# A different path for the third of the last four token tiles, and a finer cut of the last one

## The chip, the cores and the metric

The kernel runs on one core of a Trainium2 chip. The metric is the device time of one execution in microseconds. Times "in the span" are counted from the first to the last instruction that the profile holds; the time of an execution is somewhat longer than its span.

## The reference

One encoder layer for 1024 tokens of width 1024, all in 32-bit floats. A projection feeds retention heads and windowed attention heads, their outputs go through `W_out`, and two normalisations close the two halves:

```python
h = _layer_norm(ALPHA * h + mix, ln1_gain[i], ln1_bias[i])
g = jnp.einsum('bsd,df->bsf', h, w_ffn_gate[i].astype(jnp.float32))
up = jnp.einsum('bsd,df->bsf', h, w_ffn_up[i].astype(jnp.float32))
ffn = jnp.einsum('bsf,fd->bsd', jax.nn.silu(g) * up, w_ffn_down[i].astype(jnp.float32))
...
h = _layer_norm(ALPHA * h + ffn + ple_gate * ple, ln2_gain[i], ln2_bias[i])

def _layer_norm(x, gain, bias):
    ...
    return (xf - mu) * lax.rsqrt(var + LN_EPS) * gain.astype(jnp.float32) + bias.astype(jnp.float32)
```

The change concerns only the last line: the second normalisation of some of the tokens, and the stores of its result.

## The kernel before

Tokens lie in eight tiles of 128 (tile t holds one token per partition, 1024 features along it). Each 32-bit matmul is split into three passes (lines 783 to 785). The feed-forward part is computed as a fast matrix product with fewer block products; the last of these products, `(p, s) = (4, 1)`, completes the first halves of tiles 0 to 3. Tiles 4 to 7 are complete earlier, and their normalisation (`ln2_steps`) runs beside the last matmuls.

The order on each engine is the order in which the code is written (a manual schedule for TensorE, VectorE, ScalarE, GpSimd and SyncE). Each engine works off its own queue in that order, and an instruction that waits holds up everything behind it on its engine. Stores are issued by SyncE. Transfers that add to what lies at their destination are issued by GpSimd.

The end of the program is `tail(products)`. For t = 0 to 3 it issues the matmuls of tile t's last half and then works on the normalisation, one stage behind for the tile before. The stages for a tile, with VectorE unless said otherwise:

- `addto` adds the product to the tile's accumulator `accd[t]`; for the last tile (`LAST` = 3) it also takes the half's statistics.
- `var` makes the mean and the variance; for tiles other than the last, ScalarE sums the squares.
- `rstd` adds the epsilon and takes the power -0.5 on GpSimd (line 1632) into column 15 of the tile's small table `stts[t]`.
- `center` subtracts the mean and multiplies by the gain `ln2[0]`, in two halves of 512 columns (line 1637).
- `scale` multiplies by column 15 and adds the bias `ln2[1]`, in two halves (line 1642), with a store behind each (line 1643).

For the last tiles the order is: root of tile 2, sum and statistics of tile 3, root of tile 3, scaling and stores of tile 2, centring of tile 3, scaling and stores of tile 3. `ln2_steps`, for tiles 4 to 7, already knows another way: ScalarE scales the whole tile (line 1654), VectorE multiplies by the gain (line 1657), and a transfer from GpSimd's queue adds the bias (line 1658); one store of the whole tile follows (line 1714).

Of the kernel before, what the change touches and what calls it, by code (L numbers as in the profile page):

```python
# [11 lines left out]
AF = mybir.ActivationFunctionType  # L12
ALU = mybir.AluOpType
# [29 lines left out]
def layer(tc, xT, xn, w_first, w_mt, w_rv, w_out, w_pg, w_pe, pT, w_gu, w_dn,  # L43
          consts, dec_b, dec_c, sink, gng, lnp, out):
    nc = tc.nc
    act, dve, pool, pe, sp = nc.scalar, nc.vector, nc.gpsimd, nc.tensor, nc.sync
# [213 lines left out]
    for h in range(2):  # L260
        sl = slice(h * HF, (h + 1) * HF)
        b = st[1, h]
        for g in range(2):
            a = slice(64 * g, 64 * g + 64)
# [123 lines left out]
    class Retention:  # L388
# [73 lines left out]
        def half(self, hh):  # L462
            return self.y[:, hh * HF:(hh + 1) * HF]
# [206 lines left out]
    def ytile(k):  # L670
        if ys[k] is None:
            ys[k] = a_tile([P, S], "y", "A0" if k < 4 else "A1")
        return ys[k]
# [46 lines left out]
    with tc.manual_schedule(engines={mybir.EngineType.PE}):  # L720
# [7 lines left out]
        a = Attention(0, ytile(1))  # L728
# [16 lines left out]
        for i in range(1, NPAIR):  # L745
# [3 lines left out]
            a = Attention(i, ytile(2 * i + 1))  # L749
# [22 lines left out]
    def ct(shape, tag, bufs=None, dt=F32):  # L772
        return cpool.tile(list(shape), dt, tag=tag, bufs=bufs, name=nm(tag))
# [90 lines left out]
    stts = [ct([P, 16], "stt", 8) for _ in range(NT)]  # L864
# [715 lines left out]
    hs = [slice(h * HF, (h + 1) * HF) for h in range(2)]  # L1580
    accd, R, later = [], [], []
# [24 lines left out]
    LAST = 3  # L1606
# [30 lines left out]
            dve.scalar_tensor_tensor(x, x, stts[t][:, 12:13], ln2[0][:, hs[h]], ALU.add, ALU.mult)  # L1637

    def scale(t):
        for h in range(2):  # L1640
            x = half(t, h)
            dve.scalar_tensor_tensor(x, x, stts[t][:, 15:16], ln2[1][:, hs[h]], ALU.mult, ALU.add)
            sp.dma_start(out[t][:, hs[h]], x)

    def ln2_steps(t):

# [15 lines left out]
    def tail(products):  # L1662

        bs = dbank[len(SEG) - 1, GRP[4]]
        for t in range(4):
            products(t)
            if t:
                rstd(t - 1)
            addto(t, 0, bs[t], done=True)
            var(t)  # L1670
            if t < LAST:
                if t:
                    scale(t - 1)
                center(t)
        rstd(LAST)
        scale(LAST - 1)
        center(LAST)
        scale(LAST)
# [84 lines left out]
    ln2 = []  # L1763
# [191 lines left out]
```

## Time and profile before

| | |
|---|---|
| median of 3 runs | 1173.62 us (1173.25, 1173.62, and one of 4958.54) |
| profiled execution | 1174.31 us |
| its span | 1172.5 us |
| mean granted TensorE clock | 0.998 |
| TensorE busy | 1162.0 us, 99% of the span |
| VectorE busy | 892.2 us, 76% |
| ScalarE busy | 581.0 us, 50% |
| GpSimd busy | 119.5 us, 10% |
| last matmul ends, in the span | 1163.66 us |

In the profile PE is TensorE, DVE VectorE, ACT ScalarE, POOL GpSimd and SP SyncE; "SPq" rows are what SyncE's queue did. A timeline row gives start, duration, engine, line of the kernel, operation, output and inputs, shape and count; in brackets stands the idle time before it and what ended it. Rows of DMA issues end with their median time from issue to landing. The rows that the argument needs stand in the prediction.

### The profile page before, as it was taken

Reading aid. Unit: us, or ns where it says so; the run is one execution under the profiler, and the core shown is the slowest. Engines: PE = TensorE matmul, PEld = TensorE weight load, DVE = VectorE, ACT = ScalarE, POOL = GpSimd, SP = SyncE. Lnnn points to the kernel's source line nnn. Section 1 sums busy time; section 2 is a strip of 40 time slices with the busy share of each in tenths; the row PEclk is TensorE's granted clock in tenths of the full one; section 3 lists DMA queues with packets and bytes.
Section 4 is the critical chain, followed back from the end, with each engine's and each line's share of the span. In section 5 each row is a group of like instructions: output and inputs, shape, how many; then the busy total and the mean of one; then the engine's idle time right before and its main releaser. Section 6 shows DMA issues by size and latency. Waiting matters only on the chain.

```text
span 1172.5 us, 17985 instructions
## 1 busy us (share of the span) xinstructions
PE 1162.0 (99%) x6410; PEld 978.8 (83%) x6410; DVE 892.2 (76%) x1736; ACT 581.0 (50%) x1181; POOL 119.5 (10%) x181
## 2 busy tenths in 40 slices
PE   9999999999999999999999999999999999999996
PEld 7888888888888888888888888888888888888885
DVE  4666678776859788947998988888888976774677
ACT  5566347776756266213444434443344445552463
POOL 2001020202010021000000000000000011134232
PEclk9999999999999999999999999999999999999999
DMA  6345656546346945756323322332223289999977
GB/s 254 95 157 207 243 195 223 207 134 221 110 162 224 385 165 185 279 183 212 117 80 105 123 100 94 112 129 106 100 72 135 85 248 344 348 236 220 259 156 215
DMA packets 80665, 211.76 MB, mean 181 GB/s; under 512 B 9536, under 2 KB 14784, under 8 KB 80576
## 3 DMA queue, kind: packets, MB, share of 16 engines
q1 hardware_dynamic: 71936, 193.84, 47.0%
q0 software_dynamic: 8640, 16.78, 8.3%
q8 instruction: 50, 0.82, 0.3%
q14 instruction: 39, 0.32, 0.1%
HBM read 139.29 MB, written 62.13 MB: 172 GB/s over the span
## 4 chain that ended last, share of the span: by engine, by line
PE 96%; DVE 2%; DMA 1%; issue 1%; ACT 0%; DVEq 0%; POOL 0%; ACTq 0%; POOLq 0%
PE bmm L783 8%; PE bmm L784 8%; PE bmm L785 7%; PE bt L783 6%; PE bt L784 6%; PE bmm L77 6%; PE bt L785 6%; PE bmm L79 6%; PE bmm L78 6%; PE bs L785 4%; PE bs L784 4%; PE bs L783 4%; PE bo L785 3%; PE bo L783 3%; PE bo L784 3%; PE bo L565 2%
## 5 line engine op out<-in xcount | busy, mean ns | idle before, releaser
L77 PE MATMUL bmm<-H,w 128*128 128x512 f32 x240 | 97.5, 406 | 0.0
L79 PE MATMUL bmm<-H,w 128*128 128x512 f32 x240 | 94.1, 392 | 0.0
L78 PE MATMUL bmm<-H,w 128*128 128x512 f32 x240 | 94.0, 392 | 0.0
L1368 ACT ACTIVATE ev<-ev 128x512 f32<-128x512 f32 x42 | 26.4, 630 | 104.3 <-DVE ev L1397 92.8
L1542 POOL DMA_DIRECT2D h0b<-in_w_dn x24 | 21.6, 900 | 539.9 <-PE bt L785 504.6
L77 PEld LDWEIGHTS bmm<-H,w 128*128 128x128 f32 x240 | 45.2, 188 | 10.0 <-ACT H L71 0.8
L79 PEld LDWEIGHTS bmm<-H,w 128*128 128x128 f32 x240 | 45.1, 188 | 10.1
L78 PEld LDWEIGHTS bmm<-H,w 128*128 128x128 f32 x240 | 45.3, 189 | 7.9
L535 ACT ACTIVATE sc<-sc,st 128x385 f32<-128x385 f32 (+1 forms) x64 | 37.1, 584 | 16.6 <-DVE st L533 16.5
L531 DVE CUSTOM_DVE_ANT_0 sc<-cst,bs,skb 128x384 f32<-128x384 f32 (+1 forms) x64 | 34.9, 576 | 8.9 <-PE bs L530 7.7
L1397 DVE TENSOR_TENSOR ev<-ev,bt 128x512 f32<-128x512 f32 x44 | 30.1, 683 | 12.5 <-PE bt L785 12.5
L1348 DVE TENSOR_TENSOR ev<-ev,bs 128x256 f32<-128x256 f32 x63 | 25.6, 418 | 15.5 <-PE bs L785 14.7
L1370 DVE TENSOR_TENSOR ev<-ev 128x512 f32<-128x512 f32 x42 | 29.0, 691 | 10.5 <-ACT ev L1368 9.0
L72 DVE TENSOR_TENSOR w<-raw,w 128x512 fp32r<-128x512 f32 x34 | 23.1, 690 | 17.9 <-ACT w L71 17.7
L783 PE MATMUL bmm<-H,u 128*128 128x512 f32 x92 | 36.2, 393 | 0.2 <-ACT ev L1406 0.2
L784 PE MATMUL bmm<-H,u 128*128 128x512 f32 x92 | 36.1, 392 | 0.0
L785 PE MATMUL bmm<-H,u 128*128 128x512 f32 x92 | 35.8, 389 | 0.0
L541 ACT ACTIVATE sc<-sc,st 128x384 f32<-128x384 f32 (+1 forms) x64 | 34.0, 580 | 0.8 <-DVE st L539 0.8
L526 POOL COPY sc<-skb 128x1 f32<-128x1 f32 x64 | 15.1, 244 | 179.8 <-PE bt L553 159.6
L783 PE MATMUL bmm<-H,w 128*128 128x512 f32 x84 | 32.9, 392 | 0.0
L784 PE MATMUL bmm<-H,w 128*128 128x512 f32 x84 | 32.9, 392 | 0.0
L785 PE MATMUL bmm<-H,w 128*128 128x512 f32 x84 | 32.7, 389 | 0.0
(791 smaller groups left out, 3893.8 us busy)
## 6 DMA issues: line engine op xcount, KB each, us to landing
ad<-ev SPq DMA_DIRECT2D x33, 512.0 KB, 2.7
pgd<-pro SPq DMA_DIRECT2D x28, 512.0 KB, 3.0
raw<-in_w_gu SPq DMA_DIRECT2D x22, 512.0 KB, 3.6
ln<-in_w_gu SPq DMA_DIRECT2D x22, 512.0 KB, 3.9
raw<-ad SPq DMA_DIRECT2D x40, 256.0 KB, 5.9
ln<-ad SPq DMA_DIRECT2D x37, 256.0 KB, 6.3
H<-in_w_dn SPq DMA_DIRECT2D x33, 256.0 KB, 7.8
wod<-aq SPq DMA_DIRECT2D x15, 512.0 KB, 2.7
```

Source lines behind the costliest of these rows:

```text
L77: pe.matmul(o, lh, rh, start=start, stop=False)
L78: pe.matmul(o, lh, rl, start=False, stop=False)
L79: recent[0] = pe.matmul(o, ll, rh, start=False, stop=stop).ins.name
L531: dve.tensor_tensor_reduce(sc[g][:, :nk], cst[:, tc0:tc0 + nk], b[:, :nk], slope(i, g), skb[:, 2 * i + g:2 * i + g + 1], ALU.add, ALU.max, ...
L535: act.activation(sc[g][:, :nk + 1], sc[g][:, :nk + 1], AF.Exp, bias=st_[:, 1, j, g:g + 1], accum_out=st_[:, 2, j, g:g + 1])
L541: behind(act.activation(sc[g][:, :nk], sc[g][:, :nk], AF.Copy, scale=st_[:, 3, j, g:g + 1]))
L783: pe.matmul(o, lh, rh, start=start, stop=False, skip_group_check=True)
L784: pe.matmul(o, lh, rl, start=False, stop=False, skip_group_check=True)
L785: pe.matmul(o, ll, rh, start=False, stop=stop, skip_group_check=True)
L1368: act.activation(c[:, 0, :], c[:, 0, :], AF.Silu)
L1370: dve.tensor_tensor(c[:, 1, :], c[:, 0, :], c[:, 1, :], ALU.mult)
L1397: dve.tensor_tensor(get(name), ev[left][:, m, :], right, ALU.add)
```

## The change

`scale` is rewritten. Tiles 0 and 1 are treated as before. Tile 2 (`t == LAST - 1`) is multiplied by column 15 on ScalarE, whole; a transfer from GpSimd's queue adds the bias; one store of the whole tile follows. Tile 3 is scaled and stored in three pieces of 512, 256 and 256 columns. `tail`, which calls it, is unchanged.

```diff
     def scale(t):
-        for h in range(2):
-            x = half(t, h)
-            dve.scalar_tensor_tensor(x, x, stts[t][:, 15:16], ln2[1][:, hs[h]], ALU.mult, ALU.add)
-            sp.dma_start(out[t][:, hs[h]], x)
+        x = accd[t]
+        if t == LAST - 1:
+            act.activation(x, x, AF.Copy, scale=stts[t][:, 15:16])
+            pool.dma_start(x, ln2[1], accum_op=ALU.add)
+            sp.dma_start(out[t], x)
+            return
+        for a, b in ((0, 512), (512, 1024)) if t < LAST else ((0, 512), (512, 768), (768, 1024)):
+            dve.scalar_tensor_tensor(x[:, a:b], x[:, a:b], stts[t][:, 15:16], ln2[1][:, a:b], ALU.mult, ALU.add)
+            sp.dma_start(out[t][:, a:b], x[:, a:b])
```

Five lines more stand ahead of what follows, so line 1643 is 1648 in the changed kernel and line 1714 is 1719; 1642 to 1644 are the new operation, transfer and store of tile 2.

VectorE at the end of the program (`acc_8954` is tile 2, `acc_8978` tile 3, `u_9952` the gain, `u_9954` the bias):

```order
 L1622 TENSOR_SCALAR stt_3912<-stt_3912 128x1
 L1631 TENSOR_SCALAR stt_3912<-stt_3912 128x1
-L1642 SCALAR_TENSOR_TENSOR acc_8954<-acc_8954,stt_3911,u_9954 128x512 x2
 L1637 SCALAR_TENSOR_TENSOR acc_8978<-acc_8978,stt_3912,u_9952 128x512 x2
-L1642 SCALAR_TENSOR_TENSOR acc_8978<-acc_8978,stt_3912,u_9954 128x512 x2
-L1951 UNCONDITIONAL_BRANCH
+L1647 SCALAR_TENSOR_TENSOR acc_8978<-acc_8978,stt_3912,u_9954 128x512
+L1647 SCALAR_TENSOR_TENSOR acc_8978<-acc_8978,stt_3912,u_9954 128x256 x2
+L1956 UNCONDITIONAL_BRANCH
```

The pair for tile 2 is gone, and the last pair is cut in three.

GpSimd at the end of the program (the four rows at the top are the roots of tiles 0 to 3):

```order
 L1632 TENSOR_TENSOR stt_3909<-stt_3909,cst 128x1
 L1632 TENSOR_TENSOR stt_3910<-stt_3910,cst 128x1
 L1632 TENSOR_TENSOR stt_3911<-stt_3911,cst 128x1
 L1632 TENSOR_TENSOR stt_3912<-stt_3912,cst 128x1
-L1951 UNCONDITIONAL_BRANCH
-L1951 ISA
+L1643 DMA acc_8954<-u_9954 128x1024
+L1956 UNCONDITIONAL_BRANCH
+L1956 ISA
```

The adding transfer for tile 2 stands behind the root of tile 3.

SyncE at the end of the program, before (stores of tile 7 and then of tiles 0 to 3, two halves each):

```order
L1714 DMA out_y<-acc_9110 128x1024
L1643 DMA out_y<-acc_8899 128x512 x2
L1643 DMA out_y<-acc_8926 128x512 x2
L1643 DMA out_y<-acc_8954 128x512 x2
L1643 DMA out_y<-acc_8978 128x512 x2
L1951 UNCONDITIONAL_BRANCH
```

and with the change:

```order
L1719 DMA out_y<-acc_9110 128x1024
L1648 DMA out_y<-acc_8899 128x512 x2
L1648 DMA out_y<-acc_8926 128x512 x2
L1644 DMA out_y<-acc_8954 128x1024
L1648 DMA out_y<-acc_8978 128x512
L1648 DMA out_y<-acc_8978 128x256 x2
L1956 UNCONDITIONAL_BRANCH
```

The store of tile 2 is one, and it stands ahead of the three of tile 3. ScalarE gets the scaling of tile 2 as its last instruction.

## The prediction

> **What bounds the kernel now.** I read the page first, then the end of the timeline engine by engine, then the DMA views of the same stretch, since the change touches only the last steps of the program.
>
> ```profile
> span 1172.5 us, 17985 instructions
> PE 1162.0 (99%) x6410; PEld 978.8 (83%) x6410; DVE 892.2 (76%) x1736; ACT 581.0 (50%) x1181; POOL 119.5 (10%) x181
> PE 96%; DVE 2%; DMA 1%; issue 1%; ACT 0%; DVEq 0%; POOL 0%; ACTq 0%; POOLq 0%
> ```
>
> TensorE is busy for 99% of the span and carries 96% of the chain that ended last. The diff has no matmul in it and nothing that a matmul waits for, so that part keeps its length. What can move is what comes after the last matmul.
>
> ```profile
> 1163.27 0.39 PE L785 MATMUL bs<-u,u 128*128 128x512 f32 x1
> ```
> ```profile
> 1163.69 0.69 DVE L1600 TENSOR_TENSOR acc<-acc,bs 128x512 f32<-128x512 f32 x1 [0.17 <-PE bs L785]
> 1164.41 0.69 DVE L1602 BATCH_NORM_STATS2 stt<-acc 128x6 f32<-128x512 f32 x1
> ...
> 1165.46 0.14 DVE L1631 TENSOR_SCALAR stt<-stt 128x1 f32<-128x1 f32 x1
> 1165.52 1.40 DVE L1642 SCALAR_TENSOR_TENSOR acc<-acc,stt,u 128x512 f32<-128x512 f32 x2
> 1166.84 1.41 DVE L1637 SCALAR_TENSOR_TENSOR acc<-acc,stt,u 128x512 f32<-128x512 f32 x2
> 1168.16 1.41 DVE L1642 SCALAR_TENSOR_TENSOR acc<-acc,stt,u 128x512 f32<-128x512 f32 x2
> ```
>
> The last product ends at 1163.66. From there the end is a chain on VectorE without a gap: the last tile's sum and statistics, then three pairs of half-tile operations: scaling of tile 2 (L1642), centring of tile 3 (L1637), scaling of tile 3 (L1642 again), ending at 1169.57. Behind it stands one store:
>
> ```profile
> 1169.60 0.33 SPq L1643 DMA_DIRECT2D out_y<-acc  x1
> ```
> ```profile
> out_y<-acc SPq DMA_DIRECT2D x2, 256.0 KB, 2.0
> ```
>
> The last half-tile store is issued at 1169.60 and lands 2.0 us later, at 1171.6; the span ends at 1172.5, so 0.9 us lie between the last landing and the end. About 8.8 us of the span follow the last matmul, and this is all that the change can act on. The time of this profiled execution is 1174.31, 1.81 above its span; the median of the runs is 1173.62, 1.12 above the span. I make the sum in the span and add 1.12.
>
> **The change, part by part.** First, what goes. The pair at 1165.52 leaves VectorE. Centring of tile 3 starts where it stood, so all that VectorE does behind it comes 1.32 us earlier (1166.84 less 1165.52). The reciprocal root of tile 3 on GpSimd, which its scaling needs, keeps its place:
>
> ```profile
> 1142.14 0.91 POOL L1658 DMA_DIRECT2D acc<-u  x1 [0.36 <-DVE stt L1630]
> 1142.79 1.92 POOL L1632 TENSOR_TENSOR stt<-stt,cst 128x1 f32<-128x1 f32 x1
> ...
> 1150.32 0.89 POOL L1658 DMA_DIRECT2D acc<-u  x1 [3.17 <-DVE acc L1657]
> 1151.46 0.86 POOL L1658 DMA_DIRECT2D acc<-u  x1 [0.25 <-issue]
> 1163.60 0.54 POOL L1632 TENSOR_TENSOR stt<-stt,cst 128x1 f32<-128x1 f32 x1 [3.53 <-DVE stt L1631]
> 1165.68 0.98 POOL L1632 TENSOR_TENSOR stt<-stt,cst 128x1 f32<-128x1 f32 x1 [1.55 <-DVE stt L1631]
> ```
>
> It ends at 1166.66, and the earlier centring would end at about 1166.9, so it is in time, by 0.2 us. Its 0.98 beside VectorE's pair (against 0.54 for the one at 1163.60) I keep, since VectorE runs the same kind of pair beside it; 0.54 and 1.92 are the bounds, -0.4 and +0.9.
>
> The last scaling is cut into 512, 256 and 256 columns. No row shows this operation at 256 columns; the nearest is
>
> ```profile
> L1348 DVE TENSOR_TENSOR ev<-ev,bs 128x256 f32<-128x256 f32 x63 | 25.6, 418 | 15.5 <-PE bs L785 14.7
> ```
>
> 0.42 us against 0.74 for a half tile. VectorE would end between 1168.3 and 1169.0; I take 1168.4. If the stores followed at once, this alone would bring the end forward by about 1 us.
>
> Second, what comes in its place, and it is on another path. ScalarE scales all of tile 2 in one operation. Like rows and the end of its work before:
>
> ```profile
> 1147.19 1.24 ACT L1654 ACTIVATE acc<-acc,stt 128x1024 f32<-128x1024 f32 x1 [0.93 <-POOL stt L1651]
> ...
> 1161.99 0.18 ACT L1615 ACTIVATION_READ_ACCUMULATOR sg<-acc,stt 128x1 f32 x1
> ```
>
> ScalarE is idle from 1162.2. The operation needs tile 2 centred (1163.2) and tile 2's root (1163.60 + 0.54 = 1164.14), so it runs from 1164.2 to 1165.4. It costs nothing, because the next step is held until 1167 anyway; without that cover it could be 1.6 us later before it counted.
>
> The next step is the adding transfer of the bias into tile 2, issued by GpSimd. It stands in GpSimd's order behind the root of tile 3, although it needs nothing of it. So it cannot start before 1166.66; the rows above show 0.25 to 0.41 us between an operation and such an issue, and I take 0.4: start at 1167.05. How long it takes until it has landed:
>
> ```profile
> L1658 POOL DMA_DIRECT2D acc<-u x4: 859/894/913, 1142.1 to 1151.5; - x4
> DMA to landing us min/median/max: 4.6/4.9/6.7
> ```
> ```profile
> q0 software_dynamic: 124, 0.51, 66.5%
> ```
> ```profile
> 1146.79 0.34 SPq L1714 DMA_DIRECT2D out_y<-acc  x1
> ```
>
> This is the same transfer (the same bias tile, 512 KB, into a tile of the same size), four times. The first, issued at 1142.14, ran with nothing else in flight (in the DMA view of 1142 to 1146 only the software queue moved data) and took 4.6; its tile's store was issued at 1146.79, 4.65 after the adding transfer's issue. The 6.7 is for the fourth, beside stores and the third. What lies beside the new one:
>
> ```profile
> core 0: us, PE busy (x) PEld busy (x) DVE busy (x) ACT busy (x) POOL busy (x), PEclk, DMA share, GB/s
> 1164.20:1165.50 1.30, 0.00 (x0) 0.00 (x0) 1.20 (x5) 0.00 (x0) 0.00 (x0) 1.00 0.00 0
> 1165.50:1166.90 1.40, 0.00 (x0) 0.00 (x0) 1.40 (x5) 0.00 (x0) 0.98 (x1) 1.00 0.00 0
> ```
>
> The DMA engines are empty, and the two stores that would have filled them next are the ones that the change removes. So I take 4.65, with 6.7 as the upper bound: the store of tile 2 is issued at 1167.05 + 4.65 = 1171.70. That is already 2.1 us after the issue of the last store of the kernel before.
>
> The Trainium skill, "DMA: Bandwidth & Descriptors", section "Anatomy of one DMA — SWDGE (gpsimd) path", gives for a transfer issued by GpSimd 2.0 us plus its bytes at 436 GB/s. By that the landing would be an estimated 3.2 us and the end 1.4 us earlier; the four rows of 4.6 and more decide against it for an adding transfer.
>
> Third, the queue behind it. SyncE issues the stores in written order: all of tile 2 first, then the three pieces of tile 3. So the pieces, whose data is ready at 1168.4, wait behind tile 2's semaphore. That SyncE's queue stands still for such a transfer the profile of before shows already:
>
> ```profile
> SPq L1714 <- DMA acc<-u: 36.7, 4, 26.4
> ```
>
> From 1171.70 there are 1 MB to store in four transfers.
>
> ```profile
> L1714 SPq DMA_DIRECT2D out_y<-acc x4: 332/336/338, 1146.8 to 1158.2; - x4
> DMA to landing us min/median/max: 2.7/3.2/4.5
> ```
> ```profile
> raw<-in_pT SPq DMA_DIRECT2D x8, 128.0 KB, 2.5
> ```
>
> A whole tile lands 2.7 us after its issue where nothing is beside it, a half tile 2.0, so 256 KB more cost 0.7. Issues cost 0.33 each and lie ahead of the data, so the bytes set the end: 2.7 for tile 2, 0.7 for the first piece, and 0.35 for each 128 KB piece if the price goes with bytes, 0.7 if it goes with the number of rows, which is as large as for a half tile. I take 0.35: a whole tile's store and a half tile's have the same 128 rows and yet differ by 0.7, so there the bytes carry the price. The last landing is 1171.70 + 2.7 + 0.7 + 0.7 = 1175.8. Bounds: not before the last issue (1172.7) plus 2.0, which is 1174.7, and not after 1176.5 by this reckoning; the 2.5 of a 128 KB load lies between.
>
> The sum: 1175.8 plus the 0.9 behind the last landing gives a span of 1176.7, that is 4.2 us more than 1172.5. With 1.12 added, the time is **1177.8**.
>
> **The rivals.** (a) *The adding transfer's issue is held up by VectorE.* The root under the long VectorE operation took 1.92 instead of 0.54, so VectorE can hold GpSimd up, and VectorE is busy without a gap until 1168.4. If the issue waited for that, it would start 1.3 us later and everything behind it too: span 1178.0, time 1179.1. Against it speaks this row beside the issue at 1150.32:
>
> ```profile
> 1148.70 2.34 DVE L1657 TENSOR_TENSOR acc<-acc,u 128x1024 f32<-128x1024 f32 x2
> ```
>
> That issue ran inside the second of the two long operations and took 0.89, as the undisturbed ones. I give it 0.12. The Trainium skill, "SBUF — State Buffer", section "SBUF: two separate sides", states a rule for this: VectorE operations in a two-port mode keep GpSimd from writing its descriptors, while those with two SBUF inputs block only GpSimd operations that read SBUF. The 1.92 and the 0.89 agree with the second half of it; no row here shows an issue beside a two-port operation.
>
> (b) *The software queue is slow again,* as for its loads with addition:
>
> ```profile
> DMA to landing us min/median/max: 4.1/6.8/9.7
> ```
>
> These are 256 KB each at line L1542, amid a full DMA. With 9.7 instead of 4.6 the span would be 1181.8 and the time 1182.9. The empty DMA engines speak against it: 0.05.
>
> (c) *Not slower: the adding transfer does not decide.* If tile 2's store were away before the pieces of tile 3 are ready, the end would be VectorE's: the last piece is issued at about 1168.6, lands 2.0 to 2.5 later, and the span is 1171.5 to 1172.0, a time of 1172.6 to 1173.1. It decides as soon as the adding transfer lands before about 1168.3, which is 1.3 us after its issue. The shortest such transfer, of half the bytes, speaks against it:
>
> ```profile
> DMA to landing us min/median/max: 3.4/5.7/9.5
> ```
>
> I give it 0.03. That the change does not do what it says is no case here: both new operations and the new order of stores stand on their queues.
>
> **How the numbers follow.** The forecast has 0.78, (a) 0.12, (b) 0.05, (c) 0.03; 0.02 is left for something not seen here. The likeliest gives 1177.8. The bounds of its terms are -0.4 and +0.9 (the root), +2.1 (a landing of 6.7), -1.1 and +0.7 (the stores), with some 0.4 between the median and other runs. The low end, 1175.8, takes the lower bounds of the root and the stores and that 0.4 together; the high end, 1180.6, takes in (a), or a landing of 6.7 with the dearer small stores. A measurement of this kernel can tell about 2%, 23 us, from no change. For a loss of that size the adding transfer would have to take some 24 us, and no case above comes near; a gain of that size is more than all that follows the last matmul. So within 2% has 0.96, slower by more 0.03, faster by more 0.01.
>
> **What would show it right or wrong.** In the profile of the changed kernel: ScalarE's new operation at about 1164.2 for 1.24 us; VectorE ending near 1168.4; GpSimd's adding issue starting at 1167.0 to 1167.1 and landing 4.6 later; four SyncE issues close together from 1171.7, the pieces of tile 3 more than 3 us after VectorE finished them; the last landing near 1175.8. It is wrong if SyncE issues the pieces before tile 2's store, if the adding transfer lands in under 2 us, or if its issue starts only when VectorE is done. A shift of the last matmul's end from 1163.66 would mean that the change acts elsewhere than I say.

## The result and the profile after

The changed kernel takes 1177.79 us (median of 6 runs, 1176.95 to 1179.0), the kernel before 1173.43 beside it (six runs, one of them of 4958.54 and left out of the ratio). The ratio is 1.0035, with a 95% interval of 1.0025 to 1.0045: slower by about 4.1 us, 2.9 to 5.3, clear of the noise but far within 2%. The profiled execution took 1178.98 us.

Here and below I use the **tail**: the span less the end of the last matmul, with the span as the page gives it, to a tenth, so that a difference of 0.1 between two tails says nothing. Before it was 1172.5 less 1163.66, 8.84 us. The first rows are the span and the last matmul of the changed kernel, from its page and its timeline:

```profile
span 1177.2 us, 17987 instructions
```
```profile
1164.03 0.39 PE L785 MATMUL bs<-u,u 128*128 128x512 f32 x1
```

The last matmul ends at 1164.42, so the tail is 12.78 us, 3.94 more. The other 0.76 us of the longer span lie ahead of the tail, where nothing was changed; more on that behind the experiments. The rows of the tail, engine by engine (VectorE, ScalarE, GpSimd, SyncE), from the timeline:

```profile
1166.34 1.42 DVE L1637 SCALAR_TENSOR_TENSOR acc<-acc,stt,u 128x512 f32<-128x512 f32 x2
1167.67 1.54 DVE L1647 SCALAR_TENSOR_TENSOR acc<-acc,stt,u 128x512 f32<-128x512 f32 x3
```
```profile
1164.93 1.15 ACT L1642 ACTIVATE acc<-acc,stt 128x1024 f32<-128x1024 f32 x1 [1.99 <-POOL stt L1632]
```
```profile
1166.45 1.05 POOL L1632 TENSOR_TENSOR stt<-stt,cst 128x1 f32<-128x1 f32 x1 [1.54 <-DVE stt L1631]
1167.46 0.90 POOL L1643 DMA_DIRECT2D acc<-u  x1
```
```profile
1172.08 0.33 SPq L1644 DMA_DIRECT2D out_y<-acc  x1
1172.50 1.89 SPq L1648 DMA_DIRECT2D out_y<-acc  x3
```

VectorE is done 1169.21, that is 4.79 us into the tail instead of 5.91. But no store of tile 3 leaves then: SyncE's queue stands at tile 2's store until 1172.08, and the three pieces leave behind it. The waits of SyncE's queue name the reason (waited for, total, times, longest), and the DMA view of the tail gives the landings (KB each, median time from issue to landing):

```profile
SPq L1644 <- DMA acc<-u: 9.0, 1, 9.0
```
```profile
acc<-u POOLq DMA_DIRECT2D x1, 512.0 KB, 4.6
out_y<-acc SPq DMA_DIRECT2D x1, 512.0 KB, 2.6
out_y<-acc SPq DMA_DIRECT2D x1, 256.0 KB, 3.0
out_y<-acc SPq DMA_DIRECT2D x2, 128.0 KB, 2.7
```

ScalarE's scaling, which the change added, ended 1.4 us before GpSimd's issue and cost nothing.

### The profile page after: what moved, and what is told of

It is laid out like the page before. It is cut to its first block, busy times and chain, and to the rows that moved or that the text cites. A ratio compares the mean times of both kernels' runs of the same rounds, so it can differ in the third digit from the quotient of the medians.

```text
span 1177.2 us, 17987 instructions
## 1 busy us (share of the span) xinstructions
PE 1162.4 (99%) x6410; PEld 979.2 (83%) x6410; DVE 891.5 (76%) x1735; ACT 582.7 (49%) x1182; POOL 120.3 (10%) x182
## 4 chain that ended last, share of the span: by engine, by line
PE 95%; DVE 2%; DMA 1%; issue 1%; ACT 0%; SPq 0%; POOL 0%; DVEq 0%; ACTq 0%; POOLq 0%
PE bmm L783 8%; PE bmm L784 7%; PE bmm L785 7%; PE bt L783 6%; PE bt L784 6%; PE bt L785 6%; PE bmm L77 6%; PE bmm L79 6%; PE bmm L78 6%; PE bs L785 4%; PE bs L784 4%; PE bs L783 4%; PE bo L785 3%; PE bo L783 3%; PE bo L784 3%; PE bo L565 2%
```

## The experiments

The theories: A, tile 2's adding transfer and the order of SyncE's queue behind it set the end. B, the small stores of the cut are what costs. C, VectorE holds up the adding transfer's issue. D came up on the way and concerns the end of the program. All diffs are against the changed kernel unless said otherwise. The tail and the end of the last matmul are those of one profiled execution each; the time is the median of several. The ratios are to runs of the kernel before beside each (medians 1174.11 to 1174.38), so the times go by the ratios and not by the first row:

| run | last matmul ends | tail, us | time, us | ratio to before, 95% interval |
|---|---|---|---|---|
| before | 1163.66 | 8.84 | 1173.43 | |
| before_again | 1163.62 | 8.88 | 1174.3 | one run |
| the change | 1164.42 | 12.78 | 1177.79 | 1.0035 [1.0025, 1.0045] |
| t3_first | 1163.08 | 11.22 | 1176.12 | 1.0018 [1.0008, 1.0028] |
| add_early | 1162.59 | 11.81 | 1177.14 | 1.0024 [1.0015, 1.0034] |
| both_orders | 1162.98 | 10.22 | 1175.78 | 1.0011 [1.0002, 1.0020] |
| no_bias | 1163.77 | 7.83 | 1173.37 | 0.9993 [0.9983, 1.0002] |
| no_cut | 1164.02 | 12.58 | 1178.38 | 1.0037 [1.0024, 1.0050] |
| cut_alone | 1163.92 | 9.48 | 1174.85 | 1.0005 [0.9996, 1.0014] |
| nine_stores | 1163.75 | 9.35 | 1174.59 | 1.0001 [0.9992, 1.0010] |
| cut_eight | 1163.98 | 9.12 | 1174.36 | 1.0002 [0.9993, 1.0011] |
| add_to_hbm | 1163.62 | 9.68 | 1175.11 | 1.0009 [1.0000, 1.0018] |
| half_moved | 1163.99 | 9.41 | 1174.67 | 1.0003 [0.9994, 1.0012] |
| half_two | 1165.82 | 8.88 | 1174.37 | 1.0001 [0.9992, 1.0010] |

**SyncE's order alone (t3_first).**

```diff
-            sp.dma_start(out[t], x)
             return
...
         center(LAST)
         scale(LAST)
+        sp.dma_start(out[LAST - 1], accd[LAST - 1])
```

> Only the order on SyncE's queue is changed against the change: tile 3's three stores are issued ahead of tile 2's. The measure is the tail, from the end of the last matmul to the end of the span: 8.84 us before, 12.78 with the change. Theory A (tile 2's adding transfer and, behind it, SyncE's queue set the end): the three stores leave near 4.9 us into the tail, tile 2's store still waits until about 7.7, lands 2.6 later, and the tail is 11.2, time about 1.6 us below the change. Theory B (the three small stores themselves are what costs): the small stores still cost their time but early, so the same 11.2; it parts from A only in the run without the cut. Theory C (the adding transfer is late because VectorE holds up its issue): no change of the issue, tail as in A.

The tail is 11.22, as expected. The order of the queue was worth 1.56 of the 3.94 us. Tile 2's store is now the last: it leaves 7.63 into the tail, and its 2.7 us and the 0.9 behind it make the rest:

```profile
1170.71 0.33 SPq L1683 DMA_DIRECT2D out_y<-acc  x1
out_y<-acc SPq DMA_DIRECT2D x1, 512.0 KB, 2.7
```

**GpSimd's order alone (add_early).**

```diff
-        rstd(LAST)
         scale(LAST - 1)
+        rstd(LAST)
         center(LAST)
         scale(LAST)
```

> Only GpSimd's order is changed against the change: tile 2's adding transfer is issued ahead of tile 3's root instead of behind it. Theory A: the issue moves from 3.04 us into the tail to about 1.7 (ScalarE's end), everything behind it by as much, tail 11.4 against 12.78; tile 3's root comes some tenths later and is still in time or costs VectorE less than 0.5, which does not show at the end. Theory C (VectorE holds up the issue): the issue of 0.9 us becomes longer or the landing grows beyond 4.6, since VectorE is in its pair for tile 3 then too, and the tail stays above 12.

The tail is 11.81, not 11.4; the gain is 0.97 instead of 1.4. The issue came 0.4 us after ScalarE's end, for which I had allowed nothing, and tile 3's root behind it kept VectorE waiting for 0.46, which does not show at the end:

```profile
1164.66 0.90 POOL L1643 DMA_DIRECT2D acc<-u  x1 [1.59 <-ACT acc L1642]
1165.27 1.08 POOL L1632 TENSOR_TENSOR stt<-stt,cst 128x1 f32<-128x1 f32 x1
```
```profile
1166.39 1.54 DVE L1647 SCALAR_TENSOR_TENSOR acc<-acc,stt,u 128x512 f32<-128x512 f32 x3 [0.46 <-POOL stt L1632]
```

Theory C falls: the issue, here wholly inside VectorE's centring of tile 3, takes 0.90 and the landing 4.6, as in the changed kernel, where VectorE goes from that pair to the scaling.

**Without the adding transfer (no_bias).**

```diff
             act.activation(x, x, AF.Copy, scale=stts[t][:, 15:16])
-            pool.dma_start(x, ln2[1], accum_op=ALU.add)
             sp.dma_start(out[t], x)
```

> Tile 2 gets no bias here: the adding transfer is left out, ScalarE's scaling and the one store stay. Theory A: without the adding transfer VectorE sets the end, 1.3 us earlier than before; the last small store leaves 4.9 us into the tail and lands 2.0 to 2.5 later, tail 7.8 to 8.3 against 8.84 before, time 0.5 to 1 us below the kernel before. Theory B (the small stores cost what VectorE gains): tail 8.8 or more.

The tail is 7.83, 1.0 us below before. So the earlier VectorE does bring the end forward, if nothing stands in SyncE's way; the last small store left 0.14 us after VectorE's end and landed as fast as a half tile's did before:

```profile
1168.69 0.40 SPq L1647 DMA_DIRECT2D out_y<-acc  x1
out_y<-acc SPq DMA_DIRECT2D x1, 128.0 KB, 2.0
```

This kernel leaves out tile 2's bias, so it is no version to use; the whole gain of the change, had the bias been free, is this 1.0 us. In time the ratio 0.9993 fits it but does not tell it from nothing.

**The move alone (no_cut) and the cut alone (cut_alone).** no_cut keeps the move and stores tile 3 in halves; cut_alone keeps the cut and lets VectorE scale tile 2 as before.

```diff
-        for a, b in ((0, 512), (512, 1024)) if t < LAST else ((0, 512), (512, 768), (768, 1024)):
+        for a, b in ((0, 512), (512, 1024)):
```

> Only the move of tile 2 is kept; tile 3 is scaled and stored in two halves as before. Theory A: the move carries the whole loss, tail 12.4 to 12.8 against 12.78 with the change and 8.84 before. Theory B (the cut carries a good part of the loss): tail under 12, 11 if it carries half.

```diff
-        if t == LAST - 1:
+        if t == -1:
             act.activation(x, x, AF.Copy, scale=stts[t][:, 15:16])
```

> Only the cut of tile 3 into three pieces is made; tile 2 is scaled by VectorE and stored in halves as before. Theory A: VectorE takes 0.13 us more for three pieces than for two, the last store has half the bytes (0.35 less) but lands up to 0.5 later than its bytes say: tail 8.5 to 9.2 against 8.84 before, no difference in time. Theory B (the cut costs): tail 9.5 or more.

The move alone has a tail of 12.58, so it carries 3.74 of the 3.94; B falls as the cause of the loss. Its last store, the second half of tile 3:

```profile
1172.57 0.74 SPq L1648 DMA_DIRECT2D out_y<-acc  x1
out_y<-acc SPq DMA_DIRECT2D x1, 256.0 KB, 3.1
```

But the cut alone was not free: 9.48, outside A's 8.5 to 9.2 and at B's bound of 9.5. VectorE ended 0.13 later and SyncE's third issue came behind the second, so the last landing is 0.2 us later; the rest, 0.4, lies behind it. The last store:

```profile
1170.10 0.40 SPq L1648 DMA_DIRECT2D out_y<-acc  x1
out_y<-acc SPq DMA_DIRECT2D x1, 128.0 KB, 2.0
```

That store landed at 1172.1, yet the span ends at 1173.4, 1.3 later and not 0.9. The instructions of the program's end (line 1956, in the kernel before 1951) on SyncE's queue from the last landing on show why (count, ns each, first and last start); first the cut alone, then the kernel before:

```profile
L1956 SPq EVENT_SEMAPHORE  x8: 27/28/28, 1172.1 to 1172.6; - x8
```
```profile
L1951 SPq EVENT_SEMAPHORE  x1: 28/28/28, 1171.6 to 1171.6; - x1
```

SyncE waits for its eight transfer semaphores one after the other, about 0.06 us each. Before, the last store's semaphore was the last in that order and one wait was left when it landed; with one store more the last store seems to come back to the first, and all eight waits follow its landing. That is theory D, and two runs test it.

**The number of stores (nine_stores, cut_eight).** nine_stores is the kernel before with tile 0's first store in two pieces (its diff is against the kernel before); cut_eight is cut_alone, with its line, and tile 0 stored whole (only what it has beyond cut_alone is shown).

```diff
             x = half(t, h)
             dve.scalar_tensor_tensor(x, x, stts[t][:, 15:16], ln2[1][:, hs[h]], ALU.mult, ALU.add)
-            sp.dma_start(out[t][:, hs[h]], x)
+            if t == 0 and h == 0:
+                for q in (slice(0, 256), slice(256, 512)):
+                    sp.dma_start(out[t][:, q], accd[t][:, q])
+            else:
+                sp.dma_start(out[t][:, hs[h]], x)
```

> The kernel before with one edit far from the end: the first half of tile 0 is stored in two pieces, so that the last eight stores become nine. Theory D (the end of the program waits for SyncE's eight transfer semaphores one after the other, 0.06 us each, in a fixed order, and a ninth store comes back to the first of them): the last landing stays near 7.97 us into the tail, and what follows it grows from 0.91 to about 1.33, tail 9.3 against 8.88. Rival (the longer end of the cut runs came from the small last stores): tail 8.9.

```diff
-            sp.dma_start(out[t][:, a:b], x[:, a:b])
+            if t:
+                sp.dma_start(out[t][:, a:b], x[:, a:b])
+        if t == 0:
+            sp.dma_start(out[t], x)
```

> The cut of tile 3 alone, as in the run of that edit, but tile 0 stored whole, so that there are eight stores again. Theory D: what follows the last landing is 0.91 again instead of 1.34, last landing 8.2, tail 9.1 against 9.53. Rival (small last stores): tail 9.5.

Tails of 9.35 and 9.12, and the waits behind the last landing are eight and one:

```profile
L1955 SPq EVENT_SEMAPHORE  x8: 27/28/28, 1171.8 to 1172.2; - x8
```
```profile
L1959 SPq EVENT_SEMAPHORE  x1: 28/28/28, 1172.2 to 1172.2; - x1
```

D holds in both directions: with the ninth store at tile 0, more than 10 us ahead of the end, the tail is 0.5 us longer than before, and without it the cut alone loses 0.36 and costs 0.28. The changed kernel has eight stores for tiles 0 to 3 (two, two, one and three), so it does not pay this. The times show neither difference.

**The kernel before again (before_again).**

> The kernel before once more, for the scatter of its parts: the tail should be 8.84 within 0.1 us, while the end of the last matmul (1163.66 in the first profile, 1164.42 with the change) may move by a microsecond from run to run. If it comes back at 1163.7, the 0.76 us that the changed kernel was later there belongs to the change or to its profiled execution; if it lies between or beyond, it is scatter.

It came back at 1163.62 with a tail of 8.88. In the six profiles without the new GpSimd transfer the last matmul ends between 1163.62 and 1163.98; in the eight with it, between 1162.59 and 1165.82, to both sides of the kernel before. The executions that were not profiled say what the 0.76 is. Those of the changed kernel have spans of 1175.2 to 1177.2, median 1176.0, and the profiled one is among the two longest; half_two's, with 1165.82, was the slowest of its 11 too, 2.15 above its median. If the tail is the same in all of them, as 8.84 and 8.88 suggest for the kernel before, 1163.2 of the changed kernel's median span lie ahead of it, no more than before. So the 0.76 is most likely scatter between executions; why one execution takes longer than another ahead of the tail stays open.

**Versions that might beat both (add_to_hbm, half_moved, half_two, both_orders).** add_to_hbm stores the bias to tile 2's place in the output early and adds the scaled tile onto it:

```diff
             act.activation(x, x, AF.Copy, scale=stts[t][:, 15:16])
-            pool.dma_start(x, ln2[1], accum_op=ALU.add)
-            sp.dma_start(out[t], x)
+            pool.dma_start(out[t], x, accum_op=ALU.add)
             return
...
+                sp.dma_start(out[LAST - 1], ln2[1])
                 while later:
                     pop()
```

and has GpSimd's order of add_early.

> A version that may beat both: the bias is stored into tile 2's place in the output early, and GpSimd's adding transfer puts the scaled tile straight onto it, ahead of tile 3's root; tile 2 needs no store of SyncE's at the end. Theory A: the adding transfer is issued near 1.8 us into the tail and lands 4.6 to 5.5 later, before the last small store of tile 3, which leaves near 5.2; tail 7.8 to 8.5, time 0.3 to 1 us below the kernel before. If adding into memory off the core takes over 6 us, the tail is 8.8 or more and nothing is won.

The tail is 9.68, a miss. The adding transfer took 5.4, as allowed for, and had landed in time, but tile 3's root, behind it on GpSimd, kept VectorE waiting for 0.46, and tile 3's stores ran beside it and took 3.2 to 3.5 instead of 2.0:

```profile
out_y<-acc POOLq DMA_DIRECT2D x1, 512.0 KB, 5.4
```
```profile
1169.15 0.45 SPq L1647 DMA_DIRECT2D out_y<-acc  x1
out_y<-acc SPq DMA_DIRECT2D x1, 128.0 KB, 3.2
```

half_moved sends half of tile 2 along the new path, with its store last; half_two does the same, but stores tile 3 in halves and puts the moved half's store between them. Both have GpSimd's order of add_early; the diff is the part of `scale` that they share.

```diff
-            act.activation(x, x, AF.Copy, scale=stts[t][:, 15:16])
-            pool.dma_start(x, ln2[1], accum_op=ALU.add)
-            sp.dma_start(out[t], x)
+            y = half(t, 1)
+            act.activation(y, y, AF.Copy, scale=stts[t][:, 15:16])
+            pool.dma_start(y, ln2[1][:, hs[1]], accum_op=ALU.add)
+            y = half(t, 0)
+            dve.scalar_tensor_tensor(y, y, stts[t][:, 15:16], ln2[1][:, hs[0]], ALU.mult, ALU.add)
+            sp.dma_start(out[t][:, hs[0]], y)
             return
```

> Only half of tile 2 takes the new path (ScalarE, adding transfer of 256 KB issued ahead of tile 3's root), VectorE scales the other half, and the moved half's store is the last on SyncE's queue. Theory A: the issue is near 1.3 us into the tail, landing 3.4 to 4.6 later, its store leaves near 5.7 behind tile 3's pieces, tail 8.2 to 9.0 against 8.84 before: a gain of half a microsecond at best. If a half tile's adding transfer takes as long as a whole one's with VectorE busy, tail 9 or more.

> Half of tile 2 on the new path with its adding transfer ahead of tile 3's root, tile 3 in two halves, and the moved half's store between the two stores of tile 3: eight stores. Theory A with D: VectorE ends 5.25 us into the tail instead of 5.92, the moved half has landed at 5.0, the last store leaves at 5.4 to 5.5 and lands at 7.5, tail 8.4 against 8.88; in time a gain of 0.5 us, which 5 rounds may not resolve. If the last two stores or the adding transfer disturb each other by more than 0.5, tail 8.9 or more.

Tails of 9.41 and 8.88, both misses. half_moved has nine stores, so that by D it pays 0.4 us, which its expectation did not reckon with; without that it would stand at the upper end of what was expected. half_two pays elsewhere: VectorE ended 5.26 us into the tail, 0.65 earlier than before, and the last store left 0.41 earlier, but it landed 2.5 after its issue instead of 2.0, behind the moved half's store:

```profile
1170.87 0.38 SPq L1653 DMA_DIRECT2D out_y<-acc  x1
out_y<-acc SPq DMA_DIRECT2D x1, 256.0 KB, 2.3
```
```profile
1171.35 0.41 SPq L1651 DMA_DIRECT2D out_y<-acc  x1
out_y<-acc SPq DMA_DIRECT2D x1, 256.0 KB, 2.5
```

Three half-tile stores left within 0.9 us; by the prediction's prices, 2.0 for the first and 0.7 for each further one, the last lands 3.4 after the first issue, and 3.4 is what it took (1170.45 to 1173.85). So what VectorE saves is given back to the transfers.

both_orders joins t3_first and add_early:

> The change with both orders mended: adding transfer ahead of tile 3's root and tile 2's store behind tile 3's. Theory A: the adding transfer lands 6.6 into the tail as in the run with that order alone, tile 2's store leaves at 6.7 and lands 2.7 later, 0.9 follows: tail 10.3 against 12.78 with the change and 8.88 before, time still 1 to 1.5 us above before. So no order makes the whole-tile adding transfer pay: its 4.6 and the store behind it are longer than what VectorE saves.

The tail is 10.22, made up as expected:

```profile
1169.65 0.33 SPq L1683 DMA_DIRECT2D out_y<-acc  x1
out_y<-acc SPq DMA_DIRECT2D x1, 512.0 KB, 2.7
```

None of the orders of the whole-tile adding transfer that were run reaches the kernel before, and no complete version run here has a shorter tail or a ratio below 1.

## Why the prediction was right

The mechanism was right as well as the number: the adding transfer, held behind tile 3's root, set the end, and SyncE's queue stood behind it. Step by step, with times counted into the tail (the prediction's less 1163.66, the measured less 1164.42).

- VectorE freed: its end was put at 4.74 and came at 4.79. A 256-column piece takes 0.48 where I took 0.42 from another operation; the row of the changed kernel's three pieces (ns each: least, median, most) is

```profile
L1647 DVE SCALAR_TENSOR_TENSOR acc<-acc,stt,u x3: 480/481/747, 1167.7 to 1168.7; 128x256 f32<-128x256 f32 x2, 128x512 f32<-128x512 f32 x1
```

- The earlier end this would bring by itself was put at about 1 us; no_bias shows 1.0.
- ScalarE's scaling was put at 0.5 for 1.24 us and came at 0.51 for 1.15. Its cover held.
- The adding transfer's issue was put at 3.39 and came at 3.04. Tile 3's root took 1.05 (0.98 taken), but the 0.4 us that I put between it and the issue were not there: the issue began as the root ended. Of the terms of the sum this is the largest miss, 0.35. The 0.4 does appear in add_early, where the issue waits for ScalarE.
- Its landing was put at 4.65 with the store's issue, and took 4.62.
- The four stores were put at 4.1 from the first issue to the last landing. The last piece left at 1173.80 and landed 2.5 later, 4.2 after 1172.08:

```profile
1173.80 0.59 SPq L1648 DMA_DIRECT2D out_y<-acc  x1
out_y<-acc SPq DMA_DIRECT2D x1, 128.0 KB, 2.5
```

  The price of an issue was wrong: the issues were not 0.33 apart but 0.42, 0.47 and 0.83, and the third itself took 0.73. The profile of before had such rows, a third store in a row at 1159.15 with an issue of 0.74. Why issues grow longer behind others no run shows. The sum came out all the same, as the prediction said that the bytes set the end: in no_cut the same bytes in three stores landed 4.0 after the first issue, as four do in 4.2.
- Behind the last landing 0.9 were put, and 0.9 came.

The change stayed within 2%, to which the prediction gave 0.96. The tail was forecast at 13.04 and is 12.78: 3.94 us more than before against 4.2. That the time agrees to 0.01 us is luck: the measured difference is known only to 2.9 to 5.3, and the executions of the changed kernel lie up to 2 us apart. The 1.12 added to the span is no constant of the kernel either, but a median time less the span of one slower execution; an execution takes about 1.8 more than its own span (1178.98 against 1177.2). The sum holds because it is a difference of 4.2 added to a median. Its low end should be 1175.9 by its own terms, not 1175.8. Of the signs of being wrong, one appeared: the last matmul ended 0.76 later than 1163.66, but the spans above point to scatter and not to the change. Of the 3.94, the runs assign 1.56 to SyncE's order, 0.97 to GpSimd's order and 0.20 to the cut, each taken alone; both orders mended together take off 2.56 and leave 1.38 over before, which is the adding transfer and the store behind it.

Rival (a) was refuted: the issue began at 1167.46, 1.75 us before VectorE was done, and took 0.90, and the landing came after 4.6. (The issue at 1150.32 that the prediction set against it ended at 1151.21, 0.17 after VectorE's operation, so it lay inside it for the most part and not wholly.) The rule that I weighed there, of the Trainium skill ("SBUF — State Buffer", section "SBUF: two separate sides"), agrees with the runs in its half on operations with two SBUF inputs: tile 3's root, which reads SBUF, took 1.05 beside VectorE's two-input pair, where tile 2's took 0.54 without such a pair, and the issue was not slowed. No run here shows an issue beside a two-port operation. Rival (b) was refuted by the 4.6. Rival (c) would have needed the adding transfer to land 1.3 us after its issue; in no_bias, without it, VectorE did set the end.

## What to carry to other kernels

Taking work off the engine that ends last pays only if what replaces it is shorter than the work left on that engine: here 1.3 us of VectorE were replaced by a chain of 4.6 us of adding transfer and 2.6 of store. Look at every queue that the new step is put on: a transfer that waits holds up the stores written behind it, and writing it ahead of or behind an unrelated instruction moved the end by 1.0 and 1.6 us. In the last microseconds, count stores and bytes: here 1 MB was still to be stored when the adding transfer had landed, and it took 4.2 us.

## What the runs showed of the hardware that was not expected

- The end of the program depends on which semaphore the last transfer uses. One store more or less at tile 0, far ahead, moved the tail by 0.4 to 0.5 us (nine_stores 9.35 against 8.84; cut_eight 9.12 against 9.48), as it does if SyncE's eight semaphores are used in turn.
- Plain stores issued while an adding transfer was in flight landed only after it. In t3_first the three stores of tile 3 took 4.2 to 4.3 us, as in the row below, where they need 2.0 to 2.1 in no_bias; the adding transfer took its 4.6 all the same. The first store behind it landed 0.6 to 0.7 us after it in all five runs that have such a pair at the end, whether issued 0.9 us (half_moved, half_two), 1.0 (t3_first) or 2.5 (both_orders, add_to_hbm) behind the adding issue. In t3_first, from 1167.2 to 1170.4, the adding transfer moved 0.52 MB and the stores 0.08. It holds the other way round too: in the kernel before, the adding transfer issued at 1150.32, 0.27 us behind a whole tile's store, took 5.3. What sets this order no run shows.

```profile
1168.11 1.20 SPq L1647 DMA_DIRECT2D out_y<-acc  x1
out_y<-acc SPq DMA_DIRECT2D x1, 128.0 KB, 4.2
```

- An adding transfer of half the bytes took 3.4 us in half_moved against 4.6 for the whole, so 256 KB cost 1.2 us there; a plain store of 256 KB more costs 0.7.
